# Side programs of the two mixers: one step per tick, one recurrence block at a time, GpSimd's large operations on other engines

## The chip, the cores and the metric

The kernel runs on one core of a Trainium2 chip. The core has five engines that take their instructions in order, each from its own queue: TensorE (PE, matmuls; its weight loads are shown as PEld), VectorE (DVE), ScalarE (ACT), GpSimd (POOL) and SyncE (SP, which here only issues DMAs; POOL and ACT issue some too). An instruction whose data is not ready holds up all that stand behind it in its queue. The metric is device microseconds of one execution; lower is better.

## The reference, cut to what matters

One layer over 256 prompt tokens and 8 x 4 sample tokens (288 columns, all in fp32), d_model 2048: a feed-forward block, a mixer, a second feed-forward block, each with a residual and a layer norm.

```python
x = layer_norm(DEEP_ALPHA * x + 0.5 * swiglu(x, w['ffn1_w_in'], w['ffn1_w_out']), w['ln1_g'], w['ln1_b'])
proj = x @ w['w_mix_in']
y_s5, n_re, n_im = s5_mixer(proj[..., :S5_WIDTH], s5_re, s5_im, w)
y_gdn, n_s, n_buf = gdn_mixer(proj[..., OFF_QKV:OFF_GATE], proj[..., OFF_GATE:OFF_BETA],
                              proj[..., OFF_BETA:OFF_DECAY], proj[..., OFF_DECAY:MIX_IN_COLS],
                              gdn_s, conv_buf, w)
mix = jnp.concatenate([y_s5, y_gdn], axis=-1) @ w['w_mix_out']
x = layer_norm(DEEP_ALPHA * x + mix, w['ln2_g'], w['ln2_b'])
x = layer_norm(DEEP_ALPHA * x + 0.5 * swiglu(x, w['ffn2_w_in'], w['ffn2_w_out']), w['ln3_g'], w['ln3_b'])
```

`s5_mixer` is a complex diagonal recurrence over 64 groups of 16 channels, then a gelu and a gated product with `s5_glu_w`. `gdn_mixer` runs a short causal convolution over q, k and v, then a gated delta rule with 8 heads of 128 x 128 state; the prompt does it in chunks, the samples start from a state of their own that is read from and written back to memory.

## The kernel before, in words

**Main work.** Every large product is split into three matmuls: the weights are loaded from memory in chunks of 128 x 4 x 256 (512 KB), ACT rounds a chunk to `whi` (L116), DVE subtracts to get `wlo` (L119), and PE runs, for each k, hi x hi (L123), hi x lo (L124) and lo x hi (L125) with 288 columns. A chunk is 24 such matmuls, called mains below. `raw`, `whi` and `wlo` have three buffers each. All weight loads (L115) are issued by SP, which takes its DMAs in order too.

**Side programs.** While the mixer's products run, the other work of the mixer goes on beside them as Python generators. `launch(gen, rate)` puts one on a list; `tick()` is called after every 12 mains of a wide product and gives each of them `rate` steps (up to the next `yield`). So the rate says how densely a side program's instructions are written between the mains. A scheduler then orders the instructions of each engine from what was written; what came out is what each engine runs.

- `gates()` (rate 3): decays and betas of the delta rule, many small operations on a 128 x 24 tile.
- `s5(f)`, f = 0 to 7 (rate 1.5, two at a time, `SF = Slots(2)`): one block of the recurrence. It loads its tables (`btd`, `rtd`, `cad`, `tzd`) and its input `ud` (8 DMAs, L819) from SP, runs 32 small matmuls (L840), a scan on DVE (L853), 64 + 64 small matmuls (L871, L874), writes `yd` and reads it back in another layout with 8 DMAs from SP (L884), then does the gelu.
- `conv(...)`: the short convolution of each head.
- `prompt_pair(pr)`, pr = 0 to 3 (rates 1.3, 1.3, 2, 2.5): two heads of the delta rule for the prompt; some 25 steps that go from PE to DVE or ACT and back (L1047 is its helper for 32 x 32 products).
- `sample(hg)`, two of them (rates 0.85 and 2): the same for the samples, after all s5 blocks are done (`while not s5done`); it shares the PSUM bank `sx` with s5.
- `update(bk)` (rate 2): the new states of the samples, 16 tiles of 128 x 512 that are loaded, scaled by GpSimd (L1353) or ACT (L1356), increased by a product (L1366, L1370) and stored.

The order of the mixer's products is a string at L1449: v and h are values and heads of a pair, d two blocks of s5 input, g gates, s the launch of a sample program. Then come the product with `s5_glu_w`, and `w_mix_out` in two halves; the second half runs beside `update` and the second layer norm, whose sums GpSimd keeps for the first 12 tiles (L259, L264, L265).

In this stage GpSimd also does every fourth weight split (`turn[1] = 4`).

Of the kernel before, what the change touches and what calls it, by code (L numbers as in the profile page):

```python
# [16 lines left out]
N = 288  # L17
# [6 lines left out]
CL = 8  # L24
# [38 lines left out]
def body(tc, x_prompt, x_sample, state_s5_re, state_s5_im, state_gdn, state_conv,  # L63
# [45 lines left out]
    turn = [0, 0]  # L109

    def split(src):
        raw = wp.tile([128, 4, 256], F32, name="raw", bufs=3)
        hi = wp.tile([128, 4, 256], F32R, name="whi")
        lo = wp.tile([128, 4, 256], F32R, name="wlo")
        D.dma_start(raw, src)  # L115
        S.activation(hi, raw, AF.Copy)  # L116
        turn[0] += 1
        e = G if turn[1] and turn[0] % turn[1] == 0 else V
        e.tensor_sub(lo, raw, f32(hi))  # L119
        return hi, lo  # L120
# [186 lines left out]
    rtd = dr.tile([128, 2, 32, NC], F32, name="rtd")  # L307
# [10 lines left out]
    MAG, MAGC, A4 = cols[:, 0], cols[:, 1], cols[:, 2:4]  # L318
# [3 lines left out]
    with tc.tile_pool(name="f1", bufs=1) as fp:  # L322
# [73 lines left out]
        def s5_setup():  # L396
# [114 lines left out]
            G.dma_start(rtd, cs[:, :, :, CL + 1:])  # L511
# [9 lines left out]
            G.tensor_copy(MAGC, mp[:, :, CL])  # L521
# [133 lines left out]
    with tc.tile_pool(name="mix", bufs=1) as mp:  # L655
# [5 lines left out]
        def s5t(dt=F32):  # L661
            return mp.tile([128, 2 * N], dt, name="s5", bufs=8)
# [14 lines left out]
        def gates():  # L677
# [96 lines left out]
            for b in range(5):  # L774
# [14 lines left out]
                G.tensor_mul(em[:, :n], em[:, :n], bc(M("le" + sfx), n))  # L789
# [9 lines left out]
        HB = [mp.tile([128, 8, CS + 1], F32, name=f"HB{i}") for i in range(2)]  # L799
# [4 lines left out]
        SF = Slots(2)  # L804
# [4 lines left out]
        def s5(f):  # L809
            yield from SF.take()  # L810
            H, q0 = HB[f % 2], 4 * f
# [5 lines left out]
            D.dma_start(rt, rtd[:, :, q0:q0 + 4])  # L817
            for j in range(CL):
# [5 lines left out]
            G.tensor_tensor(dec, C("reset")[:, None, None, :].to_broadcast([128, 4, 2, NC]),  # L824
                            MAGC[:, q0:q0 + 4, None, None].to_broadcast([128, 4, 2, NC]), op=OP.mult)
            for ri in range(2):
                for g2 in range(2):
                    G.tensor_copy(H[64 * ri:64 * ri + 64, g2::2, :8].rearrange("p q b -> p b q"),
                                  H0[64 * g2:64 * g2 + 64, ri, 1:, q0:q0 + 4])
# [28 lines left out]
            G.tensor_mul(m2, h, sin)  # L858
# [5 lines left out]
            G.tensor_copy(FH[:, 8 * f:8 * f + 8], H[:, :, CS])  # L864
# [26 lines left out]
            G.tensor_mul(b, b, a)  # L891
# [47 lines left out]
        def conv(psum, mt, out, outs, sem):  # L939
# [5 lines left out]
            G.tensor_copy(sm[:, :, 0:3], SC[:, mt].rearrange("p (b j) -> p b j", j=3))  # L945
# [3 lines left out]
            G.tensor_copy(CBT[:, mt].rearrange("p (s x) -> p s x", x=3),  # L949
                          buf[:, 256:319].rearrange("p (s x) -> p s x", x=7)[:, :, 0:3])  # L950
# [10 lines left out]
        LP, ST, SS = [Slots(1), Slots(1)], Slots(1), Slots(7)  # L961
# [19 lines left out]
        def delta(qt, kt, vt, mi0, n, ATT, levels, col, vdone, bk, par):  # L981
# [44 lines left out]
            G.tensor_mul(wt, gd, bc(C("m1t"), n))  # L1026
            G.tensor_add(wt, wt, bc(C("id32"), n))
# [218 lines left out]
        def sample(hg):  # L1246
# [13 lines left out]
            while not s5done:  # L1260
                yield

            yield from SS.take()
# [3 lines left out]
            for a in range(2):  # L1267
                G.tensor_copy(kq[:, :, a], KQS[:, a, 4 * hg:4 * hg + 4].rearrange("p h (f n) -> p (h f) n", n=16))
            for h2 in range(2):
                yield from bk.take()  # L1270
                p = grid(bk(), 4)
                for i in range(4):
                    h, hf = 2 * h2 + i // 2, i % 2
                    yield from SS.take()
                    s0 = state(hg, h, hf)
                    yield
                    yield
                    for b in range(4):
                        T.matmul(p[32 * b:32 * b + 32, i], kq[:, 2 * h + hf].rearrange("p a n -> p (a n)"), s0[:, b], start=True, stop=True)
                    SS.give()  # L1280
# [20 lines left out]
            SS.give()  # L1301
            yield
# [24 lines left out]
            yield from SS.take(3)  # L1327
            x, kd3, vn3 = [s5t(F32R)[:, :512].rearrange("p (a b) -> p a b", b=128) for _ in range(3)]
# [5 lines left out]
            for _ in range(4):  # L1334
                yield
# [5 lines left out]
            final[hg] = kd3, vn3  # L1341
# [311 lines left out]
```

## Time and profile before

| | |
|---|---|
| three timed runs, median | 2331.89 us (2325.61 to 2334.62) |
| the profiled execution | 2336.23 us, its span 2334.3 us |
| PE busy | 2255.2 us (97%) |
| DVE, ACT, POOL busy | 1253.6, 984.0, 536.4 us |
| first feed-forward block and layer norm | 0 to about 896 us |
| mixer | about 896 to 1463 us |
| second feed-forward block, output | to 2334.3 us |

PE's busy time is that of pipelined matmuls whose ends are modelled, so how fast it goes is read from how many matmuls start in a stretch. [...] Waits are listed by what ended them; "issue" is a wait for which the profile shows no reason.

### The profile page before, as it was taken

How to read it: one execution, taken by the hardware profiler on the slowest of the kernel's cores; microseconds unless marked ns; L12 is line 12 of the kernel's file. 1: busy time of each engine (PE TensorE's matmuls, PEld its weight loads, DVE VectorE, ACT ScalarE, POOL GpSimd, SP SyncE). 2: the span in 40 equal slices, each digit the busy share in tenths (PEclk: the TensorE clock that was granted, in tenths of full speed). 3: DMA queues.
4: the chain of work that ended last, by engine and by line, in shares of the span. 5: the costliest groups of instructions: out<-in, count | busy, mean ns of one | idle time of the engine just before them, and what ended most of it. 6: DMA issues, size and time to landing. Idle time of an engine off the chain costs nothing. (4 is left out here: it accounts for less than half of the span.)

```text
span 2334.3 us, 46725 instructions
## 1 busy us (share of the span) xinstructions
PE 2255.2 (97%) x19454; PEld 2212.9 (95%) x19454; DVE 1253.6 (54%) x1703; ACT 984.0 (42%) x1532; POOL 536.4 (23%) x798
## 2 busy tenths in 40 slices
PE   8999999999999997978999998899999999999998
PEld 8999999999999997877999998899999999999997
DVE  5566555665444457565544677654444444444444
ACT  4343343334433345444565655533334333333342
POOL 6510000000010054643532347840000000000015
PEclk9999999999999998999999999899999999999998
DMA  8565555566665545667655567455555555555553
GB/s 234 151 192 166 182 181 179 177 181 185 185 221 172 163 154 171 202 191 241 196 159 163 172 215 232 127 172 163 168 166 165 170 163 168 167 165 169 164 165 102
DMA packets 419415, 411.91 MB, mean 176 GB/s; under 512 B 43330, under 2 KB 406154, under 8 KB 418948
## 3 DMA queue, kind: packets, MB, share of 16 engines
q1 hardware_dynamic: 398288, 376.43, 52.6%
q0 software_dynamic: 11376, 29.62, 4.3%
q10 hardware_dynamic: 9540, 2.88, 0.6%
q8 instruction: 152, 2.49, 0.4%
q14 instruction: 59, 0.48, 0.1%
HBM read 380.99 MB, written 32.02 MB: 177 GB/s over the span
## 5 line engine op out<-in xcount | busy, mean ns | idle before, releaser
L119 DVE TENSOR_TENSOR wlo<-raw,whi 128x1024 fp32r<-128x1024 f32 x628 | 791.8, 1261 | 842.0 <-ACT whi L116 839.2
L123 PE MATMUL mm<-XH,whi 128*128 128x288 f32 x3760 | 1125.9, 300 | 13.8 <-ACT XH L297 9.0
L125 PE MATMUL mm<-XH,wlo 128*128 128x288 f32 x3760 | 1123.9, 300 | 14.9 <-DVE wlo L119 13.3
L124 PE MATMUL mm<-XL,whi 128*128 128x288 f32 x3760 | 1108.6, 295 | 1.0 <-POOL XL L299 0.8
L116 ACT ACTIVATE whi<-raw 128x1024 fp32r<-128x1024 f32 x648 | 685.9, 1060 | 997.9 <-PE mm L124 837.4
L123 PEld LDWEIGHTS mm<-XH,whi 128*128 128x128 f32 x3760 | 714.7, 190 | 20.8 <-ACT XH L297 9.9
L125 PEld LDWEIGHTS mm<-XH,wlo 128*128 128x128 f32 x3760 | 711.7, 190 | 18.5 <-DVE wlo L119 15.2
L124 PEld LDWEIGHTS mm<-XL,whi 128*128 128x128 f32 x3760 | 722.8, 192 | 3.3 <-POOL XL L299 1.5
L125 PE MATMUL mm<-hh,wlo 128*128 128x288 f32 x1408 | 417.1, 296 | 2.2 <-DVE wlo L119 2.2
L123 PE MATMUL mm<-hh,whi 128*128 128x288 f32 x1408 | 415.7, 295 | 1.0 <-ACT whi L116 1.0
L124 PE MATMUL mm<-hl,whi 128*128 128x288 f32 x1408 | 416.3, 296 | 0.0
L125 PEld LDWEIGHTS mm<-hh,wlo 128*128 128x128 f32 x1408 | 264.4, 188 | 3.1 <-DVE wlo L119 3.1
L123 PEld LDWEIGHTS mm<-hh,whi 128*128 128x128 f32 x1408 | 264.7, 188 | 2.0 <-ACT whi L116 1.5
L124 PEld LDWEIGHTS mm<-hl,whi 128*128 128x128 f32 x1408 | 265.1, 188 | 0.1
L259 POOL TENSOR_TENSOR lnx<-X,lnx 128x288 f32<-128x288 f32 x24 | 23.4, 976 | 890.5 <-ACT lnx L255 887.5
L614 POOL DMA_DIRECT2D cad<-cs x32 | 19.4, 643 | 260.4 <-DVE kc L626 160.5
L228 ACT ACTIVATE hh<-sg 128x288 fp32r<-128x288 f32 x88 | 38.0, 435 | 68.5 <-DVE sg L225 68.5
L119 POOL TENSOR_TENSOR wlo<-raw,whi 128x1024 fp32r<-128x1024 f32 x20 | 48.2, 2411 | 32.2 <-ACT whi L116 30.7
L239 DVE TENSOR_TENSOR X<-X,mm 128x288 f32<-128x288 f32 x96 | 42.4, 450 | 21.8 <-PE mm L125 21.6
L225 DVE TENSOR_TENSOR sg<-sg,mm 128x288 f32<-128x288 f32 x88 | 39.2, 450 | 23.0 <-PE mm L125 23.0
L606 POOL DMA_DIRECT2D btd<-cs x8 | 4.6, 579 | 196.9 <-ACT cs L605 196.9
L953 DVE SCALAR_TENSOR_TENSOR ca<-cb,CW,ca 128x312 f32<-128x312 f32 x72 | 41.2, 580 | 12.3 <-ACT ca L951 11.2
(566 smaller groups left out, 1538.4 us busy)
## 6 DMA issues: line engine op xcount, KB each, us to landing
raw<-in_ffn_w_in_dram SPq DMA_DIRECT2D x352, 512.0 KB
raw<-in_ffn_w_out_dram SPq DMA_DIRECT2D x176, 512.0 KB
raw<-in_w_mix_in_dram SPq DMA_DIRECT2D x80, 512.0 KB
raw<-in_w_mix_out_dram SPq DMA_DIRECT2D x32, 512.0 KB
cad<-cs POOLq DMA_DIRECT2D x32, 128.0 KB, 3.7
btd<-cs POOLq DMA_DIRECT2D x8, 512.0 KB, 3.7
tzd<-lag POOLq DMA_DIRECT2D x8, 512.0 KB, 10.0
big<-btd SPq DMA_DIRECT2D x8, 512.0 KB
```

What stands on the lines that cost most here:

```text
L116: S.activation(hi, raw, AF.Copy)
L119: e.tensor_sub(lo, raw, f32(hi))
L123: T.matmul(out, wh, xh, start=st, stop=False)
L124: T.matmul(out, wh, xl, start=False, stop=False)
L125: T.matmul(out, wl, xh, start=False, stop=sp)
L225: V.tensor_mul(sg, sg, ub[jj])
L228: S.activation(hh, sg, AF.Copy)
L239: V.tensor_add(X[:, m], X[:, m], b[q])
L259: e.tensor_sub(d, self.src(m), self.c)
L606: G.dma_start(btd[f], o.rearrange("p a r b -> p (a r b)"))
L614: G.dma_start(cad[f, 64 * ri:64 * ri + 64, :, g2], ca[64 * g2:64 * g2 + 64, :, ri, 16:])
L953: V.scalar_tensor_tensor(acc[:, :312], buf[:, j:j + 312], CW[:, 24 * j + mt:24 * j + mt + 1], acc[:, :312], op0=OP.mult, op1=OP.add)
```

## The change

1. The rates: gates 3 to 1.5, s5 1.5 to 1.3 and one block at a time (`SF = Slots(1)`, one `HB` tile), prompt pairs all 1, samples 0.85 and 2 to 1 and 1.4.
2. In the order of the mixer's products v1, h1, the first sample program and g0 now stand ahead of d4, so that d4 comes four products later and d6 eight. The samples no longer wait for all s5 blocks; they take their state tiles four at a time from five slots of the s5 pool (nine buffers in place of eight), one sample program at a time (`SM`).
3. Work that leaves GpSimd: the 20 weight splits, one product of the s5 step, one of the gelu, the masks of the gates and of the delta rule, 16 factors of `update` and four gathers (to DVE); the copies of `conv` and s5 and the scaling of 8 state tiles (to ACT). The decay of the scan is worked out once for all blocks during the first block and read back by two DMAs per block.
4. The loads of `kd3` and `vn3` move from the end of `sample` to the head of `update`.

By the built programs POOL has 175 instructions fewer, DVE 73 and ACT 118 more (with two table loads fewer), SP 16 DMAs more; PE has the same.

```diff
@@ -106,17 +106,13 @@
...
-    turn = [0, 0]
-
...
-        turn[0] += 1
-        e = G if turn[1] and turn[0] % turn[1] == 0 else V
-        e.tensor_sub(lo, raw, f32(hi))
+        V.tensor_sub(lo, raw, f32(hi))
@@ -304,7 +300,7 @@
...
-    rtd = dr.tile([128, 2, 32, NC], F32, name="rtd")
+    rtd = dr.tile([128, 3, 32, NC], F32, name="rtd")
@@ -518,7 +514,12 @@
...
-            G.tensor_copy(MAGC, mp[:, :, CL])
+            dec = prod()[:, :512].rearrange("p (q c) -> p q c", q=16)
+            for h in range(2):
+                G.tensor_tensor(dec, C("reset")[:, None, :].to_broadcast([128, 16, NC]),
+                                mp[:, 16 * h:16 * h + 16, CL:].to_broadcast([128, 16, NC]), op=OP.mult)
+                G.dma_start(rtd[:, 2, 16 * h:16 * h + 16], dec)
+                dec = prod()[:, :512].rearrange("p (q c) -> p q c", q=16)
@@ -659,7 +660,7 @@
...
-            return mp.tile([128, 2 * N], dt, name="s5", bufs=8)
+            return mp.tile([128, 2 * N], dt, name="s5", bufs=9)
@@ -786,7 +787,7 @@
...
-                G.tensor_mul(em[:, :n], em[:, :n], bc(M("le" + sfx), n))
+                V.tensor_mul(em[:, :n], em[:, :n], bc(M("le" + sfx), n))
@@ -796,37 +797,37 @@
...
-        HB = [mp.tile([128, 8, CS + 1], F32, name=f"HB{i}") for i in range(2)]
+        HB = [mp.tile([128, 8, CS + 1], F32, name="HB")]
...
-        SF = Slots(2)
+        SF = Slots(1)
...
-            H, q0 = HB[f % 2], 4 * f
+            H, q0 = HB[0], 4 * f
...
-            D.dma_start(rt, rtd[:, :, q0:q0 + 4])
+            D.dma_start(rt, rtd[:, :2, q0:q0 + 4])
+            for r in range(2):
+                D.dma_start(dec[:, :, r], rtd[:, 2, q0:q0 + 4])
...
-            G.tensor_tensor(dec, C("reset")[:, None, None, :].to_broadcast([128, 4, 2, NC]),
-                            MAGC[:, q0:q0 + 4, None, None].to_broadcast([128, 4, 2, NC]), op=OP.mult)
...
-                    G.tensor_copy(H[64 * ri:64 * ri + 64, g2::2, :8].rearrange("p q b -> p b q"),
-                                  H0[64 * g2:64 * g2 + 64, ri, 1:, q0:q0 + 4])
+                    S.activation(H[64 * ri:64 * ri + 64, g2::2, :8].rearrange("p q b -> p b q"),
+                                 H0[64 * g2:64 * g2 + 64, ri, 1:, q0:q0 + 4], AF.Copy)
@@ -855,13 +856,13 @@
...
-            G.tensor_mul(m2, h, sin)
+            V.tensor_mul(m2, h, sin)
...
-            G.tensor_copy(FH[:, 8 * f:8 * f + 8], H[:, :, CS])
+            S.activation(FH[:, 8 * f:8 * f + 8], H[:, :, CS], AF.Copy)
@@ -888,7 +889,7 @@
...
-            G.tensor_mul(b, b, a)
+            V.tensor_mul(b, b, a)
@@ -942,12 +943,12 @@
...
-            G.tensor_copy(sm[:, :, 0:3], SC[:, mt].rearrange("p (b j) -> p b j", j=3))
+            S.activation(sm[:, :, 0:3], SC[:, mt].rearrange("p (b j) -> p b j", j=3), AF.Copy)
...
-            G.tensor_copy(CBT[:, mt].rearrange("p (s x) -> p s x", x=3),
-                          buf[:, 256:319].rearrange("p (s x) -> p s x", x=7)[:, :, 0:3])
+            S.activation(CBT[:, mt].rearrange("p (s x) -> p s x", x=3),
+                         buf[:, 256:319].rearrange("p (s x) -> p s x", x=7)[:, :, 0:3], AF.Copy)
@@ -958,7 +959,7 @@
...
-        LP, ST, SS = [Slots(1), Slots(1)], Slots(1), Slots(7)
+        LP, ST, SS, SM = [Slots(1), Slots(1)], Slots(1), Slots(5), Slots(1)
@@ -1023,8 +1024,8 @@
...
-            G.tensor_mul(wt, gd, bc(C("m1t"), n))
-            G.tensor_add(wt, wt, bc(C("id32"), n))
+            V.tensor_mul(wt, gd, bc(C("m1t"), n))
+            V.tensor_add(wt, wt, bc(C("id32"), n))
@@ -1257,27 +1258,25 @@
...
-            while not s5done:
-                yield
-
+
+            yield from SM.take()
...
-                G.tensor_copy(kq[:, :, a], KQS[:, a, 4 * hg:4 * hg + 4].rearrange("p h (f n) -> p (h f) n", n=16))
+                V.tensor_copy(kq[:, :, a], KQS[:, a, 4 * hg:4 * hg + 4].rearrange("p h (f n) -> p (h f) n", n=16))
...
+                yield from SS.take(4)
+                s0 = [state(hg, 2 * h2 + i // 2, i % 2) for i in range(4)]
+                for _ in range(4):
+                    yield
...
-                    h, hf = 2 * h2 + i // 2, i % 2
-                    yield from SS.take()
-                    s0 = state(hg, h, hf)
-                    yield
-                    yield
...
-                        T.matmul(p[32 * b:32 * b + 32, i], kq[:, 2 * h + hf].rearrange("p a n -> p (a n)"), s0[:, b], start=True, stop=True)
-                    SS.give()
+                        T.matmul(p[32 * b:32 * b + 32, i], kq[:, 4 * h2 + i].rearrange("p a n -> p (a n)"), s0[i][:, b], start=True, stop=True)
+                SS.give(4)
@@ -1299,6 +1298,7 @@
...
+            SM.give()
@@ -1324,21 +1324,22 @@
...
-            yield from SS.take(3)
-            x, kd3, vn3 = [s5t(F32R)[:, :512].rearrange("p (a b) -> p a b", b=128) for _ in range(3)]
+            yield from SS.take()
+            x = s5t(F32R)[:, :512].rearrange("p (a b) -> p a b", b=128)
...
-            for _ in range(4):
-                yield
+
+        def parts(hg):
+            kd3, vn3 = [s5t(F32R)[:, :512].rearrange("p (a b) -> p a b", b=128) for _ in range(2)]
...
-            final[hg] = kd3, vn3
+            return kd3, vn3
@@ -1346,17 +1347,18 @@
...
             vm = mp.tile([128, 4, 128], F32R, name=vname, bufs=1)[:96]
-            G.tensor_mul(vm, f32(final[hg][1][:96, h, None, :]).to_broadcast([96, 4, 128]), C("own8")[:96, 4 * hf:4 * hf + 4, None].to_broadcast([96, 4, 128]))
+            V.tensor_mul(vm, f32(final[hg][1][:96, h, None, :]).to_broadcast([96, 4, 128]), C("own8")[:96, 4 * hf:4 * hf + 4, None].to_broadcast([96, 4, 128]))
             t = state(hg, h, hf, mp.tile([128, 4, 128], F32, name=sname, bufs=1))
             c0 = 52 + 32 * hg + 8 * h + 4 * hf
-            if hf == 0:
-                G.tensor_mul(t, t, ecol[:, c0:c0 + 4, None].to_broadcast([128, 4, 128]))
-            else:
-                for b in range(4):
-                    S.activation(t[:, b], t[:, b], AF.Copy, scale=ecol[:, c0 + b:c0 + b + 1])
+            for b in range(4):
+                S.activation(t[:, b], t[:, b], AF.Copy, scale=ecol[:, c0 + b:c0 + b + 1])
             return vm, t
...
         def update(bk):
+            for hg in range(2):
+                final[hg] = parts(hg)
+            yield
+            yield
             ahead = [factors(k, 0) for k in range(3)]
@@ -1388,15 +1390,14 @@
...
-        launch(gates(), 3)
-        turn[1] = 4
+        launch(gates(), 1.5)
...
-            launch(s5(f), 1.5)
+            launch(s5(f), 1.3)
@@ -1438,7 +1439,7 @@
...
-            launch(prompt_pair(pr, QT, KTt, vt[pr], rd[pr]), (1.3, 1.3, 2, 2.5)[pr])
+            launch(prompt_pair(pr, QT, KTt, vt[pr], rd[pr]))
@@ -1446,7 +1447,7 @@
...
-        for what in "v0 h0 d4 d6 v1 h1 g0 g2 s0 v2 h2 g4 v3 h3 g6 s1".split():
+        for what in "v0 h0 v1 h1 s0 g0 d4 g2 v2 h2 d6 g4 v3 h3 s1 g6".split():
@@ -1455,7 +1456,7 @@
...
-                launch(sample(f), (0.85, 2)[f])
+                launch(sample(f), (1, 1.4)[f])
@@ -1475,7 +1476,6 @@
...
-        turn[1] = 0
```

How it moves instructions is shown at two places. The first is SP's queue in the first half of the mixer, before: s5 blocks 2 and 3 read back `yd` (L884) and blocks 4 and 5 load their inputs (L819).

```order
51 L816 DMA big<-btd 128x1024
52 L820 DMA big<-cad 128x1024
53 L115 DMA raw<-in_w_mix_in_dram 128x4x256
54 L884 DMA s_10706<-yd 16x8x40 x8
55 L816 DMA big<-btd 128x1024
56 L820 DMA big<-cad 128x1024
57 L884 DMA s_10743<-yd 16x8x40 x8
58 L819 DMA s_11487<-ud 16x8x48 x8
59 L817 DMA s_11508<-rtd 128x2x128
60 L819 DMA s_11509<-ud 16x8x48 x8
61 L842 DMA big<-tzd 128x1024
62 L115 DMA raw<-in_w_mix_in_dram 128x4x256 x3
```

The same place of SP's queue after the change; L113 is the weight load, L885 and L822 the two of s5, L820 the new loads of the decay.

```order
46 L113 DMA raw<-in_w_mix_in_dram 128x4x256 x2
47 L843 DMA big<-tzd 128x1024
48 L817 DMA big<-btd 128x1024
49 L113 DMA raw<-in_w_mix_in_dram 128x4x256
50 L885 DMA s_10582<-yd 16x8x40 x8
51 L113 DMA raw<-in_w_mix_in_dram 128x4x256 x3
52 L823 DMA big<-cad 128x1024
53 L818 DMA s_11599<-rtd 128x2x128
54 L820 DMA s_11599<-rtd 128x4x32 x2
55 L822 DMA s_11600<-ud 16x8x48 x4
56 L113 DMA raw<-in_w_mix_in_dram 128x4x256
57 L822 DMA s_11600<-ud 16x8x48 x4
```

Before, 36 small DMAs stand between two weight loads (rows 54 to 61); after, eight, and then eight again. Over the whole mixer the longest such run is 36 before and 27 after (where block 4 reads back, block 5 loads and the first sample program reads eight pieces twice); the next longest are 20 and 17.

The second place is POOL's queue early in the mixer, where `gates()` works out the decays `G` from which the rest of the delta rule follows. Before:

```order
242 L119 TENSOR_TENSOR wlo<-raw,whi 128x1024
243 L741 TENSOR_SCALAR cb_10033<-cb_10033 128x24
244 L745 TENSOR_TENSOR cb_10033<-cb_10033 128x24
245 L864 COPY FH<-HB_9988 128x8
246 L824 TENSOR_TENSOR s_10705<-cst,cols 128x256
247 L742 TENSOR_TENSOR cb_10033<-cb_10033 128x24
248 L858 TENSOR_TENSOR s_10109<-s_10110,s_10107 128x256
249 L743 TENSOR_TENSOR cb_10033<-cb_10033 128x24
250 L746 TENSOR_TENSOR cb_10033<-cb_10033 128x24
251 L747 TENSOR_TENSOR cb_10033<-cb_10033,par 128x24
252 L748 TENSOR_SCALAR cb_10033<-cb_10033 128x24
253 L753 COPY G_9982<-cb_10033 128x2x8
```

After, with L754 for the copy to `G`:

```order
227 L745 TENSOR_SCALAR cb_10037<-cb_10037 128x24
228 L754 COPY B_9989<-cb_10037 128x2x8
229 L755 TENSOR_TENSOR sel<-cb_10037,cst 128x8
230 L742 TENSOR_SCALAR cb_10037<-cb_10037 128x24
231 L746 TENSOR_TENSOR cb_10037<-cb_10037 128x24
232 L743 TENSOR_TENSOR cb_10037<-cb_10037 128x24
233 L744 TENSOR_TENSOR cb_10037<-cb_10037 128x24
234 L747 TENSOR_TENSOR cb_10037<-cb_10037 128x24
235 L748 TENSOR_TENSOR cb_10037<-cb_10037,par 128x24
236 L749 TENSOR_SCALAR cb_10037<-cb_10037 128x24
237 L754 COPY G_9988<-cb_10037 128x2x8
```

The weight split, the copy to `FH`, the decay table and the s5 product are gone from between the steps of `gates()`.

## Rows read from the trace of the kernel before

**Rows 1.** The page, first part: PE's busy time, share and instructions.

```profile
PE 2255.2 (97%) x19454; PEld 2212.9 (95%) x19454; DVE 1253.6 (54%) x1703; ACT 984.0 (42%) x1532; POOL 536.4 (23%) x798
```

**Rows 2.** Stretches: length, busy time (instructions) of each engine, PEclk, DMA share, GB/s.

```profile
938.00:1130.00 192.00, 163.95 (x2761) 153.10 (x2759) 117.95 (x240) 93.12 (x207) 94.20 (x162) 0.92 0.69 210
1130.00:1368.00 238.00, 237.75 (x2661) 223.18 (x2660) 127.67 (x235) 141.09 (x374) 83.77 (x127) 1.00 0.59 177
1368.00:1463.00 95.00, 82.39 (x582) 78.39 (x581) 67.65 (x92) 47.63 (x90) 56.87 (x56) 0.99 0.70 212
1700.00:1800.00 100.00, 100.00 (x758) 100.00 (x757) 43.39 (x45) 39.13 (x46) 0.00 (x0) 1.00 0.54 166
```

**Rows 3.** PE's waits, 938 to 1130 us: total, times, longest.

```profile
PE g L1047 <- DVE Y L1055: 4.0, 1, 4.0
PE sx L840 <- DMA s<-ud: 3.7, 2, 2.0
PE g L763 <- POOL G L753: 3.7, 1, 3.7
PE g L1047 <- issue: 3.4, 2, 3.0
PE sx L929 <- DVE s L923: 2.1, 1, 2.1
PE sx L871 <- issue: 2.1, 1, 2.1
PE g L1087 <- ACT Y L1080: 1.7, 1, 1.7
PE mm L125 <- POOL wlo L119: 1.6, 1, 1.6
```

**Rows 4.** SP's DMA issues in order of time: start, us, what.

```profile
1030.27 4.38 SPq L884 DMA_DIRECT2D s<-yd  x8
...
1035.69 4.85 SPq L884 DMA_DIRECT2D s<-yd  x8
1040.65 3.68 SPq L819 DMA_DIRECT2D s<-ud  x8
...
1045.02 5.05 SPq L819 DMA_DIRECT2D s<-ud  x8
...
1050.64 1.52 SPq L115 DMA_DIRECT2D raw<-in_w_mix_in_dram  x3
```

**Rows 5.** ACT's waits, 938 to 1130 us: total, times, longest.

```profile
ACT whi L116 <- DMA raw<-in_w_mix_in_dram: 26.2, 7, 7.1
ACT s L888 <- DMA s<-yd: 19.9, 6, 7.4
```

**Rows 6.** POOL in order of time: start, us, operation.

```profile
959.39 2.47 POOL L119 TENSOR_TENSOR wlo<-raw,whi 128x1024 fp32r<-128x1024 f32 x1
```

**Rows 7.** DVE in order of time, the same moment.

```profile
959.83 2.19 DVE L863 TENSOR_TENSOR HB<-s 64x128 f32<-64x128 f32 x1
...
962.33 0.29 DVE L863 TENSOR_TENSOR HB<-s 64x128 f32<-64x128 f32 x1
```

**Rows 8.** Groups of DVE, 938 to 1463 us: busy, mean ns | idle before.

```profile
L119 DVE TENSOR_TENSOR wlo<-raw,whi 128x1024 fp32r<-128x1024 f32 x92 | 119.3, 1297 | 99.3 <-ACT whi L116 97.2 <-PE sx L1380 1.3 <-PE mm L124 0.7
...
L857 DVE TENSOR_TENSOR s<-s,s 128x256 f32<-128x256 f32 x8 | 5.9, 734 | 0.1
...
L1370 DVE TENSOR_TENSOR GT<-GT,g 128x512 f32<-128x512 f32 x5 | 3.4, 676 | 0.0
```

**Rows 9.** Groups of ACT, 938 to 1463 us: busy, mean ns | idle before.

```profile
L947 ACT ACTIVATE cb<-mm 128x32 f32<-128x32 f32 x24 | 4.7, 196 | 0.0
...
L1356 ACT ACTIVATE ATT<-ATT,ecol 128x128 f32<-128x128 f32 x12 | 3.8, 389 | 5.2 <-DMA ATT<-in_state_gdn_dram 5.2
```

**Rows 10.** PE's waits, 1368 to 1463 us: total, times, longest.

```profile
PE mm L123 <- ACT XH L297: 4.5, 1, 4.5
PE g L1366 <- DVE ATT L1370: 2.4, 1, 2.4
PE mm L123 <- DVE big L1500: 2.2, 1, 2.2
PE mm L125 <- DVE wlo L119: 1.9, 3, 0.9
```

More of the change, by code (lines that the diff above doesn't have):

```diff
@@ L317, in body @@
     cols = pers.tile([128, 8, 32], F32, name="cols")
-    MAG, MAGC, A4 = cols[:, 0], cols[:, 1], cols[:, 2:4]
+    MAG, A4 = cols[:, 0], cols[:, 2:4]
     H0 = pers.tile([128, 2, 9, 32], F32, name="H0")
@@ L510, in s5_setup @@
                 yield
-            G.dma_start(rtd, cs[:, :, :, CL + 1:])
+            G.dma_start(rtd[:, :2], cs[:, :, :, CL + 1:])
             mp = fp.tile([128, 32, CL + 1], F32, name="mp")
```

## The prediction, made before the changed kernel ran

> **What bounds the kernel now.** I read the page's first part, then stretches, then PE's waits in each, then the queues behind them. PE is busy 97% of the span [rows 1], so only what PE waits for, or runs slowly, can be saved. In the second feed-forward block 758 mains start in 100 us, 0.132 us each, at clock 1.00 with PE never idle [rows 2]; nothing is changed there, nor in the first block. The changed code runs from about 938 to 1463 us, and it has three parts that differ.
>
> 938 to 1130 us (gates, all eight s5 blocks, pair 0): PE is busy 163.95 of 192 us, so it waits 28.0 us, and the clock is 0.92 [rows 2]. 1130 to 1368 us (pairs 1 to 3, both samples): PE is busy 237.75 of 238 us, clock 1.00. 1368 to 1463 us (update, second norm): busy 82.39 of 95 us, 12.6 us of waits. So the loss sits where many side programs are dense, and almost none sits where pairs 1 to 3 run with a step every 22 to 25 mains of PE's queue, though DVE is as busy there (127.67 of 238 us).
>
> What ends the waits of the first part [rows 3]: GpSimd twice (3.7 and 1.6 us); twice the late landing of an s5 input (3.7); a DVE result (4.0); "issue" (3.4 and 2.1); then 2.1 and 1.7, and some 5.7 us in entries not above the last row. The 4.0 us wait for DVE has a cause further back. Between two weight loads SP issues 36 small DMAs of s5, from 1030.27 to 1050.64 us, 20.4 us or 0.57 us each [rows 4]; ACT waits 26.2 us for weights in this part and 19.9 us for `yd`, in front of the next split [rows 5], and DVE queues behind ACT. The weights have three buffers and so have their split parts: a load can run about five chunks ahead of PE, 5 x 24 x 0.132 = 15.8 us (an estimate from rows 2, without the load and split themselves). A run of 20.4 us outlasts that; one of 10 us does not.
>
> **The change part by part.** PE's instructions are the same in number and kind, so its own work costs the same; the sum is over waits, clock, and what the other engines gain.
>
> GpSimd in the gates. The 3.7 us wait is for `G`. In POOL's queue before, a weight split, an s5 product, a table and a copy stand between its steps; after, none. The split alone took 2.47 us there [rows 6], and the 1.6 us wait was for such a split too. The split goes to DVE at 1.30 us [rows 8]. Bounds of the gain 1.6 (only the wait for the split) to 5.3 us (all); I take 5, since the removed split covers most of the 3.7. Late next is the chain through ACT and DVE for the same tile, which I leave 0.3 us.
>
> SP's runs. One block at a time cuts 36 to at most 27 DMAs, and that one stands alone; others are 17 or less. At 0.57 us, 27 take 15.4 us, about the lead of the weights, and 17 take 9.7 us, well under it. A block has two more DMAs for the decay, 16 in all, 9 us of SP, within slack outside these runs. Of the 7.7 us (4.0 and 3.7) I take 5.7 as gained; bounds: 7.7, and 0 if the runs of 27 and 17 hurt as the 36 did. `ud` of block 4 is needed 48 mains after its product ends, so a wait of up to 2.0, the longest of its row, can come back there.
>
> "issue", 5.5 us. It stands before L1047 and L871, at places where side steps follow each other closely. After, steps stand further apart: I take half, 2.7; bounds 0 and 5.5.
>
> The rest of the first part, 9.5 us (2.1, 1.7 and the 5.7 not shown): half, 4.8, as two blocks no longer run beside the pair and a step of the pair has 24 mains, 3.2 us, before the next; bounds 0 and 9.5.
>
> [...]
>
> Clock. At 0.92 over 163.95 us of work, 0.08 x 164 = 13.1 us is lost. The drops come with the waits; in the next part, without waits, there is none. With under half of the waits left I take two thirds, 8.7; bounds 3 and 13.1.
>
> These add up: 5 + 5.7 + 2.7 + 4.8 + 8.7 = 26.9 us gained in what was the first part.
>
> What is added on DVE: 20 splits x 1.30 = 26; 16 s5 and gelu products x 0.73 (L857 is the same shape nearly) = 12; 16 factors x 0.68 = 11; 5 gate masks x 0.68 = 3; 16 small ones under 0.3 each, 4: 56 us. On ACT: 88 copies x 0.20 = 18 and 32 scalings x 0.39 = 12: 30 us [rows 8, 9]. Over 525 us DVE goes from 313 to 369 us busy, 60 to 70%, ACT from 282 to 312, 59%. Neither binds; but a step's DVE operation may stand behind one more split. GpSimd gives something back: while its split ran, a product of DVE took 2.19 us that took 0.29 us right after [rows 6, 7]. The cover for all this is the mains between two steps; I put 4 us of new waits in the second part, where s5 blocks and samples now also run; bounds 0 and 12.
>
> Update. PE waits 2.4 + 2.2 + 1.9 = 6.5 us there outside the norm's 4.5 [rows 10]. The factors leave GpSimd, which the second norm needs; the 8 scalings go to ACT; the last pair ends some 60 mains later, and its heads are needed about 70 mains (9 us) after. I take a gain of 1 us; bounds a loss of 5 and a gain of 4. `kd3` loads at the head of `update` stand in SP's queue over 200 mains before the first L1366, so they cost nothing; without that cover about 4 us. The decay table, two GpSimd operations and two stores during the first block, lies beside an idle GpSimd: nothing; without cover under 4 us.
>
> Sum: 26.9 - 4 + 1 = 24 us. From the profiled execution, 2336.2 us (span 2334.3 and 1.9 around it), that is 2312. The median of the runs shown is 2331.9, 4.3 lower, so the median of the changed kernel should be **2308 us**. The bounds of all terms give 2287 at best (28 us of waits, 13.1 of clock and 4 in the update gone, no new ones: 45 us) and 2344 at worst (1.6 and 3 gained, 12 and 5 lost).
>
> **The rivals.** (1) SP is still the bound: the number of s5 DMAs is larger, the run of 27 outlasts the weights' lead, and the samples' reads add to it. For it: 15.4 against 15.8 us. Against: a single run, and mains that are stretched by side steps around it. Then only GpSimd's 5 us and 3 of the clock are gained: 2324, within 0.5%.
>
> (2) DVE's queue takes over, and the kernel is slower. Steps of two pairs, a sample and an s5 block meet in the second part, some 130 between 938 and 1368 us; each goes through DVE or ACT within 3.2 us, and a split of 1.30 us, or a convolution, may be ahead. If 45 of them wait one split, that is 58 us, against 27 gained, with a clock that falls as in the first part, 3 us more: 2331.9 + 34 = 2366. It decides from about 21 such waits on (27 / 1.30). For it: 56 us more on DVE. Against: in the second part the same steps at the same distance cost PE no wait.
>
> (3) The tail: s5 block 7 and the last pair end so late that the products after them wait. Block 7's last product stands 223 mains (29 us) before the gated product, the last pair 70 mains. A wait of 8 us there gives 2316; this lies inside the forecast's own range.
>
> **How the numbers follow.** The forecast, with (3) in it, 0.66, its own range 2288 to 2324; (1) 0.18; (2) 0.16, anywhere from 2330 to 2370. Half a percent, 11.7 us, is about what a measurement tells from no change: under 2320.2 is faster, over 2343.5 slower. Faster: 0.63 of the forecast and 0.05 of (1): 0.68. Slower: 0.13 of (2). Same: the other 0.19. The range of 8 in 10 is 2288 to 2334: it leaves out some 0.14 of (2) above, and 0.05 below.
>
> **What would show it.** Right: between the second product group and the end of pair 1 PE waits less than 14 us in sum, the clock of that stretch is 0.96 or more, POOL G and wlo are gone from PE's waits, ACT's wait for weights falls from 26.2 to under 12 us. Wrong: SP's run of 27 is followed by a PE wait over 4 us (rival 1); waits of PE for DVE or ACT in small pieces summing to over 25 us in the stretch with two pairs (rival 2); a wait before the gated product or before the eighth head (rival 3).

## The result, and the profile after

The changed kernel takes 2307.91 us, the median of six runs (2302.22 to 2308.73), against 2333.11 us for the kernel before on the same chip: 25.2 us less, ratio 0.9888, 95% interval 0.9869 to 0.9907. The forecast was 2308 us. The profiled execution took 2302.22 us (span 2300.4), 34.0 us less than the one of before.

Line numbers shift by a few: the mains are L119 to L121, the split L114 (ACT) and L115 (DVE), the s5 reads L822 (`ud`) and L885 (`yd`). First the page, which answers [rows 1]:

```profile
PE 2239.4 (97%) x19454; PEld 2203.1 (96%) x19454; DVE 1265.6 (55%) x1776; ACT 1003.9 (44%) x1650; POOL 401.9 (17%) x623
```

The stretches of the changed kernel that answer [rows 2]; columns as there:

```profile
938.00:1130.00 192.00, 181.66 (x2761) 171.00 (x2760) 114.36 (x258) 116.89 (x311) 29.37 (x74) 0.97 0.70 207
1130.00:1335.00 205.00, 203.18 (x2622) 193.59 (x2622) 137.54 (x275) 128.99 (x355) 29.68 (x60) 1.00 0.71 211
1335.00:1430.00 95.00, 87.05 (x625) 83.62 (x623) 69.69 (x109) 55.60 (x117) 43.02 (x43) 0.98 0.71 220
```

In the first stretch PE runs 2761 instructions, as many as before, but is idle 10.3 us in place of 28.0, at clock 0.97 in place of 0.92. The clock is PEclk, the granted share of TensorE's full clock, as a mean over the stretch: at 1.00 the mains start 0.132 us apart [rows 2], at 0.50, as from 1479 to 1485 us of the kernel before, 0.240 us. The second is now idle 1.8 us (0.3 before), the third 8.0 (12.6 before). PE's waits in the first stretch, which answer [rows 3]:

```profile
PE g L1109 <- ACT W L1103: 4.2, 2, 2.9
PE sx L872 <- ACT SE L850: 2.8, 1, 2.8
PE g L1048 <- issue: 1.8, 1, 1.8
PE sx L875 <- issue: 0.5, 1, 0.5
```

GpSimd's results and the late `ud` are gone from the list. ACT's waits in that stretch, which answer [rows 5]:

```profile
ACT s L889 <- DMA s<-yd: 17.0, 5, 7.0
...
ACT whi L114 <- DMA raw<-in_w_mix_in_dram: 10.2, 3, 7.1
```

The wait for weights fell from 26.2 to 10.2 us; that for `yd` hardly fell. Its longest, 7.0 us, is behind PE's longest wait. SP's issues of the changed kernel in order of time there, which answer [rows 4]:

```profile
1111.65 0.57 SPq L818 DMA_DIRECT2D s<-rtd  x1
1113.61 7.49 SPq L885 DMA_DIRECT2D s<-yd  x8
1121.20 5.23 SPq L1293 DMA_DIRECT2D s<-kqd  x8
1126.47 0.99 SPq L820 DMA_DIRECT2D s<-rtd  x2
...
1127.56 4.40 SPq L822 DMA_DIRECT2D s<-ud  x8
1132.06 1.49 SPq L113 DMA_DIRECT2D raw<-in_w_mix_in_dram  x3
```

This is the forecast's run of 27: it lasts 20.3 us, 0.75 each, as long as the run of 36 did. ACT, in order of time at that place:

```profile
1122.78 0.47 ACT L889 ACTIVATE s<-s 128x320 f32<-128x320 f32 x1 [7.02 <-DMA s<-yd]
...
1124.70 0.38 ACT L1103 ACTIVATE W<-g 64x256 f32<-64x256 f32 x1
```

The gelu of s5 waits 7.02 us for `yd` at the head of ACT's queue, a split and the pair's `W` stand behind it, and PE waits 2.9 us for `W` (at 1125.13 us).

PE's waits in the update and second norm, which answer [rows 10]:

```profile
PE mm L119 <- ACT XH L293: 4.5, 1, 4.5
PE mm L119 <- ACT whi L114: 2.0, 2, 1.7
PE mm L271 <- DVE big L1521: 1.1, 1, 1.1
```

DVE groups of the changed kernel, 938 to 1460 us, which answer [rows 7, 8] (busy, mean ns):

```profile
L115 DVE TENSOR_TENSOR wlo<-raw,whi 128x1024 fp32r<-128x1024 f32 x118 | 148.0, 1255 | 101.1 <-ACT whi L114 99.3 <-DMA s<-rtd 1.3
...
L864 DVE TENSOR_TENSOR HB<-s 64x128 f32<-64x128 f32 x16 | 4.6, 288 | 0.2
...
L848 DVE TENSOR_TENSOR s<-sx,s 128x256 f32<-128x256 f32 x8 | 3.3, 415 | 0.1
```

The same two s5 groups in the kernel before, 938 to 1463 us:

```profile
L863 DVE TENSOR_TENSOR HB<-s 64x128 f32<-64x128 f32 x16 | 9.7, 606 | 0.2
...
L847 DVE TENSOR_TENSOR s<-sx,s 128x256 f32<-128x256 f32 x8 | 3.4, 421 | 2.8 <-PE sx L840 2.7
```

The subtraction of two SBUF tiles went from 606 to 288 ns on average: before, three of the 16 took 1.40 to 2.37 us and the others about 0.29, after, all did. The product that reads PSUM (`sx`) took the same before and after. Over all of DVE's work from the second product group to the end of the update I took, shape by shape, the time of operations that overlap with a computation of GpSimd above the median of those that don't: 39.1 us before, 4.7 after.

### The profile page after: what moved, and what is told of

The parts are those of the page before. It is cut to its first block, busy times and chain, and to the rows that moved or that the text cites. A ratio compares the mean times of both kernels' runs of the same rounds, so it can differ in the third digit from the quotient of the medians.

```text
span 2300.4 us, 46669 instructions
## 1 busy us (share of the span) xinstructions
PE 2239.4 (97%) x19454; PEld 2203.1 (96%) x19454; DVE 1265.6 (55%) x1776; ACT 1003.9 (44%) x1650; POOL 401.9 (17%) x623
## 4 chain that ended last, share of the span: by engine, by line
PE 84%; DMA 5%; DVE 4%; POOL 3%; issue 1%; ACT 1%; SPq 1%; ACTq 0%; DVEq 0%; POOLq 0%
PE mm L121 27%; PE mm L119 27%; PE mm L120 26%; DVE wlo L115 1%; DMA yd<-s 1%; DMA raw<-in_w_mix_in_dram 1%; DMA s<-rtd 1%; DMA raw<-in_ffn_w_out_dram 1%; DMA out_dram<-ATT 1%; ACT whi L114 0%; SPq L885 0%; DVE lnt L287 0%; PE g L1048 0%; POOL X L232 0%; DMA s<-yd 0%
## 5 line engine op out<-in xcount | busy, mean ns | idle before, releaser
L115 DVE TENSOR_TENSOR wlo<-raw,whi 128x1024 fp32r<-128x1024 f32 x648 | 813.7, 1257 | 836.4 <-ACT whi L114 834.0
L119 PE MATMUL mm<-XH,whi 128*128 128x288 f32 x3760 | 1124.5, 300 | 13.5 <-ACT XH L293 9.0
L121 PE MATMUL mm<-XH,wlo 128*128 128x288 f32 x3760 | 1120.7, 299 | 11.7 <-DVE wlo L115 11.7
L114 ACT ACTIVATE whi<-raw 128x1024 fp32r<-128x1024 f32 x648 | 685.9, 1060 | 975.3 <-PE mm L120 819.7
L119 PEld LDWEIGHTS mm<-XH,whi 128*128 128x128 f32 x3760 | 712.2, 190 | 19.0 <-ACT XH L293 9.9
L121 PEld LDWEIGHTS mm<-XH,wlo 128*128 128x128 f32 x3760 | 710.0, 189 | 13.9 <-DVE wlo L115 12.9
L121 PE MATMUL mm<-hh,wlo 128*128 128x288 f32 x1408 | 417.1, 297 | 1.9 <-DVE wlo L115 1.9
L119 PE MATMUL mm<-hh,whi 128*128 128x288 f32 x1408 | 415.7, 295 | 1.3 <-ACT whi L114 1.3
L121 PEld LDWEIGHTS mm<-hh,wlo 128*128 128x128 f32 x1408 | 264.4, 188 | 2.9 <-DVE wlo L115 2.8
L119 PEld LDWEIGHTS mm<-hh,whi 128*128 128x128 f32 x1408 | 264.7, 188 | 2.3 <-ACT whi L114 1.8
L221 DVE TENSOR_TENSOR sg<-sg,mm 128x288 f32<-128x288 f32 x88 | 39.1, 449 | 22.4 <-PE mm L121 22.3
L215 ACT ACTIVATE sg<-mm 128x288 f32<-128x288 f32 x88 | 35.3, 401 | 27.6 <-PE mm L121 27.6
L225 DVE TENSOR_TENSOR hl<-sg,hh 128x288 fp32r<-128x288 f32 x88 | 40.3, 461 | 1.5 <-ACT hh L224 1.0
```

The lines of the kernel that those rows point to most:

```text
L115: V.tensor_sub(lo, raw, f32(hi))
L119: T.matmul(out, wh, xh, start=st, stop=False)
L121: T.matmul(out, wl, xh, start=False, stop=sp)
L215: S.activation(sg, gb[jj], AF.Silu)
L221: V.tensor_mul(sg, sg, ub[jj])
L225: V.tensor_sub(hl, sg, f32(hh))
```

## Experiments

All ratios are to the kernel before, timed beside it on the same chip. The chips differ: the kernel before took 2332.7 to 2336.5 us on them, so a difference in us between kernels of different chips can be off by some 3 us, and the ratios decide. The scheduler also rearranges some small matmuls when a side program's instructions change, so some of each difference can come from the order. How much is not shown; in the last kernel below it is tens of us. Where the order is known to be nearly the same, it is said.

**GpSimd's work or the schedule?** Two halves of the change, each alone. First the moves off GpSimd in the kernel before:

```diff
-        e.tensor_sub(lo, raw, f32(hi))
+        V.tensor_sub(lo, raw, f32(hi))
...
-            G.tensor_mul(m2, h, sin)
+            V.tensor_mul(m2, h, sin)
...
-            G.tensor_copy(sm[:, :, 0:3], SC[:, mt].rearrange("p (b j) -> p b j", j=3))
+            S.activation(sm[:, :, 0:3], SC[:, mt].rearrange("p (b j) -> p b j", j=3), AF.Copy)
...
```

> The kernel before with GpSimd's work moved as in the change (splits, masks, products, factors to DVE; small copies and eight scalings to ACT); rates, order and two s5 blocks at a time stay, and so does the decay on GpSimd. Theory (the terms of the prediction): GpSimd in the gates 5 us, its share of the clock 2 to 3, update 1: about 8 us less, ratio 0.9965, with SP's run of 36 and its wait of about 4 us still there. Rival A (GpSimd was the whole cause, by its queue and by slowing DVE): 20 us or more, ratio 0.991 or less. Rival B (with steps this dense the 86 us more on DVE and ACT take over): no gain or slower, ratio 1.000 or more.

Measured 2319.10 us, ratio 0.9936 (0.9919 to 0.9952): 15.4 us, about twice the theory, less than rival A; rival B falls. Its first stretch and one wait of PE there:

```profile
938.00:1130.00 192.00, 174.39 (x2880) 165.10 (x2880) 124.64 (x288) 111.14 (x292) 40.72 (x82) 0.94 0.74 229
```

```profile
PE g L762 <- POOL G L752: 0.7, 1, 0.7
```

PE ran 119 instructions more in the stretch than before. Its waits there that name GpSimd fell from 5.3 to 0.7 us and those that name DVE from 8.3 to 0.7; those that name ACT rose from 4.2 to 7.3 and "issue" from 6.3 to 9.0. ACT waits 23.9 us for weights from 938 to 1460 us (28.0 before). DVE's extra time beside GpSimd is 4.8 us. SP's run of 36 is still there, from 1018.29 to 1037.93 us, but PE's wait of 4.0 us for DVE, which was expected with it, is not: from the run's start to 1050 us PE waits 2.8 us of "issue", 1.8 for `whi` and 0.2 for DVE.

The other half, the changed kernel with GpSimd's work put back:

```diff
-        V.tensor_sub(lo, raw, f32(hi))
+        turn[0] += 1
+        e = G if turn[1] and turn[0] % turn[1] == 0 else V
+        e.tensor_sub(lo, raw, f32(hi))
...
-            V.tensor_mul(m2, h, sin)
+            G.tensor_mul(m2, h, sin)
...
```

> The changed kernel with GpSimd's work put back (every fourth split, masks, s5 and gelu products, factors, scalings, copies; only the decay stays read from memory). Theory: 5.7 for SP's runs, 2.7 and 4.8 for issue and the rest, 6 of the clock: about 19 us less than before, ratio 0.992; the waits for GpSimd (G, wlo) are there again. Rival A (GpSimd is the whole cause): under 8 us, ratio 0.9965 or more.

Measured 2327.35 us, ratio 0.9966 (0.9954 to 0.9978): 7.1 us, as rival A had it. GpSimd's moves are the larger half: 15.4 us in the old schedule, 19.4 in the new (2327.35 against 2307.91; 18 by the ratios).

**What of GpSimd's work?** Only the splits back on GpSimd:

```diff
-        V.tensor_sub(lo, raw, f32(hi))
+        turn[0] += 1
+        e = G if turn[1] and turn[0] % turn[1] == 0 else V
+        e.tensor_sub(lo, raw, f32(hi))
...
+        turn[1] = 4
```

> The changed kernel with every fourth weight split of the mixer's first products back on GpSimd, and nothing else of its old work. All of its old work cost 19.4 us in this schedule (2327.4 against 2307.9). Theory: the splits, 20 of 2.5 us, are most of it: 12 us or more slower than the changed kernel, ratio to before 0.994 or more. Rival (the many small steps on GpSimd, G, gm, products, copies, in chains with PE): within 5 us, ratio 0.991 or less.

Measured 2317.05 us, ratio 0.9925 (0.9910 to 0.9939), between the two: the splits are 9.1 of the 19.4 us (by the ratios 9 of 18). The rest, of the many smaller operations, was not taken apart. PE's waits for GpSimd's results in the stretch are 1.6 us (`wlo` 0.9, `G` 0.7); DVE's extra time is 20.2 us.

Then work on GpSimd that nobody reads:

```diff
         V.tensor_sub(lo, raw, f32(hi))
+        turn[0] += 1
+        if turn[1] and turn[0] % turn[1] == 0:
+            G.tensor_sub(idle, idle, f32(hi[:, :, :64]))
+            for _ in range(3):
+                G.tensor_sub(idle, idle, idle)
...
+        turn[1] = 4
```

> The changed kernel with the splits on DVE as they are, and beside every fourth of them four subtractions of 128x256 on GpSimd whose result nobody reads (the first reads a piece of whi). Nothing waits for GpSimd then but its own few steps. In the kernel before, DVE's operations that overlapped with GpSimd's took 39 us more than the same shapes alone, in the changed kernel 4.7. Theory (GpSimd's cost is the slowing of DVE beside it): DVE's extra time grows by 10 us or more and the kernel by 5 us or more, ratio to before 0.9905 or more. Rival (it is the waits for GpSimd's results): within 3 us of the changed kernel, ratio under 0.990.

Measured 2314.08 us, ratio 0.9908 (0.9892 to 0.9924), 6.2 us slower than the changed kernel by the medians, 4.7 by the ratios, about what the theory had. PE's order is nearly that of the changed kernel (144 of the built program's 17675 places differ). GpSimd's groups, 938 to 1460 us (busy, mean ns), and PE's longest entry in the first stretch:

```profile
L124 POOL TENSOR_TENSOR idle<-idle 128x256 f32<-128x256 f32 x60 | 49.2, 820 | 4.0
L122 POOL TENSOR_TENSOR idle<-idle,whi 128x256 f32<-128x256 f32 x20 | 28.1, 1406 | 57.4 <-ACT whi L118 57.4
```

```profile
PE sx L884 <- DVE HB L873: 3.3, 5, 1.7
```

DVE's extra time rose from 4.7 to 18.4 us, and PE now waits for DVE's `HB`. PE's waits for GpSimd are 1.7 us (`G` 1.0, `gm` 0.7). The intervals of the two kernels overlap, so the time alone doesn't settle it; with DVE's rows I take it as the likely cause of a good part of GpSimd's 19 us.

**What of the schedule?** The old rates, then the old order of products, in the changed kernel; then one block at a time, alone, in the kernel before:

```diff
-        launch(gates(), 1.5)
+        launch(gates(), 3)
-            launch(s5(f), 1.3)
+            launch(s5(f), 1.5)
-            launch(prompt_pair(pr, QT, KTt, vt[pr], rd[pr]))
+            launch(prompt_pair(pr, QT, KTt, vt[pr], rd[pr]), (1.3, 1.3, 2, 2.5)[pr])
-                launch(sample(f), (1, 1.4)[f])
+                launch(sample(f), (0.85, 2)[f])
```

> The changed kernel with the rates of before (gates 3, s5 1.5, pairs 1.3, 1.3, 2, 2.5, samples 0.85 and 2); order of products, one s5 block at a time and GpSimd's moves stay. The schedule as a whole is worth 11 us (2319.1 against 2307.9). Theory (denser steps leave no time for each step's answer): 6 to 11 us slower than the changed kernel, ratio to before 0.9915 to 0.9935, the waits between the second product group and the end of pair 1 above 15 us. Rival (order and one block at a time are what counts): within 3 us, ratio under 0.990.

Measured 2308.87 us, ratio 0.9886 (0.9869 to 0.9903): no difference, and PE is idle 6.7 us in the first stretch where the theory had over 15. The theory falls; in this schedule the rates are worth nothing.

```diff
-        for what in "v0 h0 v1 h1 s0 g0 d4 g2 v2 h2 d6 g4 v3 h3 s1 g6".split():
+        for what in "v0 h0 d4 d6 v1 h1 g0 g2 s0 v2 h2 g4 v3 h3 g6 s1".split():
```

> The changed kernel with the order of products of before (d4 and d6 right behind pair 0, the first sample program later); one s5 block at a time and the new rates stay. The schedule is worth 11 us (2319.1 against 2307.9) and the old rates alone cost nothing. Theory (the order carries it, since it spreads the s5 blocks and their reads over pairs 1 to 3): 6 to 11 us slower than the changed kernel, ratio to before 0.9915 to 0.9935. Rival (one block at a time is enough): within 3 us, ratio under 0.990.

Measured 2300.80 us, ratio 0.9868 (0.9850 to 0.9885). The order carries nothing either; if it matters, the old one is a little better. Rates and order were not put back together.

```diff
-        SF = Slots(2)
+        SF = Slots(1)
```

> The kernel before with one s5 block at a time (two tiles stay, only one is in use at once) and nothing else changed. Theory (fewer of SP's small reads in a row): 5 to 9 us faster than before, ratio 0.996 to 0.998. Rival A (the blocks end later and the samples, which wait for all of them, end behind pair 3): slower than before, ratio over 1.002. Rival B: no change.

Measured 2320.84 us, ratio 0.9950 (0.9936 to 0.9964): 11.9 us, more than the theory. ACT's waits, 938 to 1460 us:

```profile
ACT s L888 <- DMA s<-yd: 16.7, 5, 6.5
ACT whi L116 <- DMA raw<-in_w_mix_in_dram: 12.8, 6, 7.4
```

The wait for weights falls from 28.0 to 12.8 us by this one number. PE's "issue" waits of the first stretch, 6.3 us before, are gone too, and the densest 96 mains in a row hold 388 small matmuls between them where they held 576. So shorter runs on SP and a thinner spread of s5's matmuls come together here, and which of them carries the 11.9 us is not shown. With GpSimd's 15.4 that makes 27.3, a little over the 25.2 us of the whole change; a kernel with just these two was not run. The schedule half with GpSimd's work left gained less than this one line of it (7.1 against 11.9); the intervals overlap. Its stretch 1130 to 1350 us stands beside the same stretch of the one-block kernel, first that of the schedule half:

```profile
1130.00:1350.00 220.00, 205.13 (x2595) 193.91 (x2596) 136.01 (x243) 121.47 (x311) 88.85 (x123) 0.98 0.65 193
```

```profile
1130.00:1350.00 220.00, 216.62 (x2699) 202.18 (x2697) 129.03 (x238) 129.44 (x338) 83.71 (x124) 1.00 0.62 191
```

14.9 us of idle PE against 3.4. With GpSimd's work taken off the schedule half, which is the changed kernel, 1.8 us are left: side programs spread over the second part cost waits as long as GpSimd works there, and next to none once it doesn't.

**Is it SP's small reads?** The reads doubled, the same bytes:

```diff
-                D.dma_start(uc[16 * j:16 * j + 16], ud[f].rearrange("(g h) j c -> j h g c", g=8)[CL - 1 - j])
+                for e in range(2):
+                    D.dma_start(uc[16 * j:16 * j + 16, 4 * e:4 * e + 4], ud[f].rearrange("(g h) j c -> j h g c", g=8)[CL - 1 - j][:, 4 * e:4 * e + 4])
```

> The changed kernel with each small read of an s5 block (ud, yd) cut in two on SP: 32 in place of 16 per block, the same bytes. Theory (SP's runs hold up weights and late rows of yd hold up ACT, as the gain of 11.9 us with these reads on GpSimd suggests): the loss is at least 10 us against the changed kernel, ratio to before 0.993 or more, with ACT's waits for yd and for weights grown in step. Rival (what helped there was another order of PE's small matmuls, SP has slack): within 4 us of the changed kernel, ratio 0.991 or less.

(`yd` likewise.) Measured 2341.96 us, ratio 1.0030 (1.0017 to 1.0043): 34 us slower than the changed kernel, the whole gain and more. ACT's wait for `yd`, which was to grow as well, hardly did: 18.5 us, or 24.1 with a wait of the same step that is put down to `ud`, against 22.1. Its wait for weights, 938 to 1460 us, which was 12.6 us in the changed kernel:

```profile
ACT whi L114 <- DMA raw<-in_w_mix_in_dram: 34.3, 16, 7.5
```

The reads issued by GpSimd, in the changed kernel:

```diff
-                D.dma_start(uc[16 * j:16 * j + 16], ud
+                G.dma_start(uc[16 * j:16 * j + 16], ud
...
-                D.dma_start(a[16 * g:16 * g + 16], yd
+                G.dma_start(a[16 * g:16 * g + 16], yd
```

> The changed kernel with the same small reads issued by GpSimd. Theory: the one wait left behind SP's run of 27, 2.9 us, and the 3.4 us at half clock behind it (1.7 us) go: 4 to 5 us less than the changed kernel, ratio to before 0.987. Rival: the small reads land later from GpSimd's queue, where each stands behind stores that wait for their data, and ACT waits for yd longer than 7.0 us: same or slower than the changed kernel, ratio 0.989 or more.

Measured 2295.62 us, ratio 0.9840 (0.9820 to 0.9861): 12.3 us under the changed kernel, where the theory had 4 to 5. Its first stretch, ACT's wait for weights from 938 to 1460 us, and one of GpSimd's sets of reads (0.53 us a read):

```profile
938.00:1130.00 192.00, 189.81 (x2842) 178.29 (x2841) 121.06 (x265) 123.06 (x323) 78.32 (x164) 0.99 0.76 220
```

```profile
ACT whi L114 <- DMA raw<-in_w_mix_in_dram: 6.6, 2, 6.2
```

```profile
1006.36 4.22 POOL L885 DMA_DIRECT2D s<-yd  x8
```

PE is idle 2.2 us in that stretch. Only `yd`, or the samples' `kqd` reads too:

> The changed kernel with the eight yd reads of a block on GpSimd, and the eight ud reads left on SP. Theory (a run on SP holds up weights in proportion to its length): about half of the 11 us of both, ratio to before 0.986. Rival A (it is the late yd that holds up ACT): nearly all of it, 0.984 or 0.985. Rival B (it is the reads of ud): nothing, 0.988 or more.

Measured 2302.67 us, ratio 0.9878 (0.9859 to 0.9896): between nothing and half; its interval doesn't tell it from the changed kernel. ACT's wait for weights is 16.3 us (12.6 in the changed kernel), for `yd` 3.5 (22.1). So late `yd` is not the main cost there; that weights behind the reads are fits the 6.6 us above and the 34.3 us of the doubled reads, but no run moves `ud` alone.

> The changed kernel with the small reads of s5 on GpSimd, as in the version that gave 2295.6 us, and the samples' 32 small reads of kqd there too, so that SP issues hardly any small read in the mixer. Theory (SP's runs): 1 to 4 us faster than that version, ratio to before 0.982 to 0.984. Rival (GpSimd's queue is now where they wait; each holds GpSimd about 0.53 us): same or slower, 0.984 to 0.988.

Measured 2297.52 us, ratio 0.9849 (0.9831 to 0.9868): nothing more to gain; with the samples' reads moved too it repeats the gain on another chip. Last, the reads on GpSimd with two blocks at a time (the first of these kernels, with the diff above):

> The first of these kernels, and the 8 + 8 small reads of each s5 block (ud, yd) issued by GpSimd, now nearly idle, in place of SP; SP's run of 36 is gone though two blocks still run at a time. Theory (SP's runs hold up weights): 7.7 us of waits and some 3 us of clock less than the first kernel, ratio to before 0.992. Rival (the run is hidden by the weights' lead, the waits come from dense steps): within 3 us of the first kernel.

Measured 2326.61 us, ratio 0.9961 (0.9946 to 0.9975): 7.5 us slower than without. This doesn't tell the theories apart, but shows what the order can cost. The scheduler put 647 small matmuls between the 7392nd and the 7488th main (84 in the kernel it is compared with), and there PE mostly waits, as two stretches show; until the 7296th this kernel was 30.8 us ahead, with 689 small matmuls fewer done.

```profile
1130.00:1140.00 10.00, 3.39 (x22) 2.65 (x22) 2.72 (x5) 1.81 (x7) 7.14 (x11) 0.93 0.56 181
1140.00:1150.00 10.00, 5.71 (x20) 4.11 (x20) 6.22 (x19) 2.67 (x12) 9.88 (x19) 0.50 0.51 149
```

The best of all is the changed kernel with `ud` and `yd` read from GpSimd's queue: 2295.62 us, 1.6% under the kernel before.

## Why the prediction was right, and where it was not

The time and every mark named for it came: waits 10.3 us in the first stretch (under 14 was named), clock 0.97, `G` and `wlo` gone, ACT's wait for weights 10.2 us. By stretch the sum held: waits 17.7 us less (5 + 5.7 + 2.7 + 4.8 = 18.2 predicted); clock 0.08 x 164 = 13.1 us lost before and 0.03 x 181.7 = 5.5 after, 7.6 gained (8.7); second part 1.6 lost (4); update 4.6 gained (1). That is 28.3 of the 34.0 us between the two profiled executions; the other 5.7 us don't show as waits or clock and stay open. The medians lie only 25.2 us apart, so this pair flatters the change by some 9 us. By cause the sum did not hold.

- GpSimd in the gates, 5 us with bounds 1.6 to 5.3: the term that was mis-sized. It was bounded by PE's waits that name GpSimd [rows 3]. The moves alone gave 15.4 us. GpSimd's cost stood largely under another name: DVE's operations beside it took 39.1 us too long, and PE's waits that name DVE fell by 7.6 us with the moves alone, more than those that name GpSimd (4.6). The idle work on GpSimd makes this the likely cause; its time alone doesn't settle it. The trace [rows 6, 7] had shown one such operation, 2.19 for 0.29 us, and the forecast booked it as a small something back.
- DVE's 56 us more: the stretches sum to 321.6 us after and 313.3 before, 8.3 more: DVE's extra time beside GpSimd fell by 34.4 us, which won back most of what was added. That is the likely reason why rival 2 did not come.
- SP's runs, 5.7 us, with "the rest" and the schedule's part of the clock: that SP's small reads cost time is shown in the changed kernel, by the doubled reads (34 us) and the reads on GpSimd (12.3 us). The path by which the forecast sized the term, weights late behind a run that outlasts their lead, is not the one behind the waits that it priced. The wait of 4.0 us ended 7 us into the run of 36; rows of the kernel before, ACT, DVE and PE:

```profile
1036.17 0.47 ACT L888 ACTIVATE s<-s 128x320 f32<-128x320 f32 x1 [7.36 <-DMA s<-yd]
1036.67 0.33 DVE L890 TENSOR_SCALAR s<-s 128x320 f32<-128x320 f32 x1 [6.67 <-ACT s L888]
1037.35 0.45 PE L1047 MATMUL g<-wt,Y 32*32 32x32 f32 x32 [4.03 <-DVE Y L1055]
1055.34 1.06 ACT L116 ACTIVATE whi<-raw 128x1024 fp32r<-128x1024 f32 x1 [4.98 <-DMA raw<-in_w_mix_in_dram]
```

  ACT waited for `yd`, whose eight reads open the run; DVE's gelu step waited for ACT, and the pair's `Y` stood behind it. ACT's next wait for weights ended only at 1055.34 us, and one of the two waits for `ud` (1.7 us, at 1007.46) lies before the run. With the moves alone PE's waits for `Y` and for `ud` were gone from the stretch though the run of 36 stayed. The change took 11.2 us more than the moves alone, as much as one block at a time alone (11.9 us), but what in it did so is not shown. The reason given for the end of the runs was wrong too: the run of 27 did not shrink to 15.4 us, it took 20.3. Rival 1 was half right: its mark, a PE wait over 4 us behind that run, stayed at 2.9, again by way of `yd`, but SP's reads were still worth 12.3 us.
- Rates and order of the products: the forecast gave them a part of "issue" and "rest"; put back one at a time they cost nothing; both at once were not put back.
- "Issue": 5.5 us in the rows shown before, 6.3 in all, to 2.3; half was predicted. With PE's instructions the same in number it was 9.0 us with the moves alone and none with one block at a time alone; two rows of the first of these:

```profile
PE mm L123 <- issue: 4.1, 2, 2.2
PE g L1046 <- issue: 3.9, 1, 3.9
```

  So it follows how the side programs are laid out. What stands behind it in the hardware, no run shows.
- Update: idle 12.6 to 8.0 us, more than taken. The wait behind a sum of DVE, 2.4 us [rows 10], is gone in the kernel with GpSimd's moves alone and still 2.5 us in the one with one block at a time alone: it went with the moves; that the factors were the part of them that counted is likely, not shown.

Mis-sized terms of both signs met in a right sum: GpSimd, about 8 us with its share of the clock and the update, came to 15.4, the schedule, about 19, to 7.1 alone and 11.2 on top of the moves. That the two errors cancelled is luck.

## What to carry to other kernels

Size an engine's cost not by the waits that name it alone, but by what the same shapes on its neighbour take with and without it beside them: here DVE's operations beside GpSimd took 39.1 us too long, against 5.3 us of PE's waits that name GpSimd in the first stretch. Before a wait is priced, follow it in order of time to the head of each queue: the wait of 4.0 us came by way of `yd`, not of weights. A queue that loads the main stream's weights should not issue dozens of small reads: count them between two weight loads, and give them to a queue with slack: here twice as many cost 34 us, and GpSimd's queue in place of SP's gained 12.3. When several knobs are turned at once, turn each back: here one number (`Slots(1)`) and the work off GpSimd, each alone, sum to all of it, and the rates and the order, each alone, to nothing.

## What the hardware showed that was not expected

In the kernel before, some of DVE's operations on SBUF tiles alone were slowed beside GpSimd's, those with a PSUM operand were not: `HB<-s` took 606 ns on average there and 288 in the changed kernel, `s<-sx,s` 421 and 415. From 938 to 1430 us of the kernel before, among shapes seen both ways, 35 of 133 two-tile operations in SBUF that overlapped with GpSimd took over 1.3 times their shape's median without it, and none of 62 with a PSUM operand. Three of 14 with one tile and a scalar did too. The operation of 2.19 us beside a split of 2.47 us [rows 6, 7] ended 0.16 us after the split; what held it up is not shown. A small read took GpSimd 0.53 us to issue where `ud` and `yd` are read from its queue; on SP, in the changed kernel, it took 0.45 to 0.94 us by sets, 0.58 on average, so GpSimd's queue was no dearer for them.
